# The last hidden chunk of each feed-forward as eight block products, and RWKV's key made after its triangular inverse

## Chip, core and metric

One core of one Trainium2 chip. The kernel is a single program; its time is what the device takes for one execution, in microseconds (us). TensorE (PE) multiplies matrices, VectorE (DVE) does elementwise arithmetic, ScalarE (ACT) copies and activations, GpSimd (POOL) a few small powers and masks, and SyncE (SP) issues the loads from HBM. Each works through its own queue in a fixed order and waits for the others by semaphores.

## What is computed

A decoder trunk of four layers on 256 tokens of width 1024, in float32. Each layer is a feed-forward, a token mixer and a second feed-forward, each between two RMS norms:

```python
for layer in range(DEPTH):                       # 4
    g = norm_g[layer]
    ff = swiglu(rmsnorm(h, g[0]), ffn_w_in[layer, 0], ffn_w_out[layer, 0])
    h = h + 0.5 * rmsnorm(ff, g[1])
    u = rmsnorm(h, g[2])
    m = mixer(u)          # sliding-window attention, GLA, RWKV-7, sliding-window attention
    h = h + rmsnorm(m, g[3])
    ff = swiglu(rmsnorm(h, g[4]), ffn_w_in[layer, 1], ffn_w_out[layer, 1])
    h = h + 0.5 * rmsnorm(ff, g[5])
```

`swiglu(x)` is `(silu(gate) * up) @ w_out` with `gate, up = split(x @ w_in)` and 2816 hidden columns. In RWKV-7 the key that the change moves is `k = k * (1 + (a - 1) * k_a)`, where `a` is a sigmoid of a low-rank product.

## The kernel before

The twelve stages are called 0a, 0 mixer, 0b, 1a and so on to 3b: layer, then first feed-forward, mixer, second feed-forward. The 256 tokens are two tiles of 128. Float32 products go through TensorE as three passes (`mm3`): every operand is split into a rounded high part (an ACT copy) and the rest (a DVE subtraction), and high x high, high x low and low x high are added up in PSUM.

**Feed-forward (`ffn`).** The hidden columns come in 11 chunks of 256 (`NCH`). The first three (`OLD`) go tile by tile (`tokens`), the others as *up blocks*: for each half chunk, 48 matmuls of 256 columns give gate and up for both tiles in one PSUM bank, ACT takes the SiLU, and one DVE multiplication, the *gate* (`m<-ps,hf` in the profile), makes the hidden values and frees the bank. The down product of a chunk is a 2x2 block product (two hidden halves by two output halves, for two tiles) that Strassen's scheme in Winograd's form does in seven products of three 512-column matmuls instead of eight. Each of the seven has its own PSUM bank, `acc[1]` to `acc[7]`, in which it is summed over the chunks; up blocks use the eighth bank. The scheme needs sums of blocks: `weights` makes four differences of a chunk's weight tiles and splits seven tiles, `hidden` makes four sums of hidden blocks and splits seven.

Products 1, 6, 5, 2 (`FIRST`) and 3 make tile 0's two output halves: `c1[0] = acc1 + acc2`, `c1[1] = acc1 + acc6 + acc5 + acc3`. Products 7 and 4 are wanted for tile 1 alone: in the last `TAIL` chunks they are done after tile 0's sums are recorded. `postnorm(0)` squares `c1` on ACT, multiplies it by the output norm's gain on DVE, takes a power on POOL and adds to the residual `h`; the next stage begins with a norm of `h` and TensorE transposes of it. The gain is loaded by `gain` (a row sent to all 128 partitions, 256 KB each half) and scaled on DVE (`TENSOR_SCALAR m<-m`).

**RWKV (`rwkv_unit`).** Four units, two tiles by two halves of the heads. Each makes decays, `kk`, `bt`, the key `kn` and its scaled form `kt` on DVE; then transposes, products and a triangular inverse built up over levels m = 2 to 64, in which DVE adds PSUM blocks; then `kt` is transposed (`bk[1]`) and its products with the queries' side are made.

**What sets the order.** Nothing is issued as it is written. `Recorder` records all operations with a key (TensorE work recorded so far, `base + rate * pe + shift`) and a price; `schedule` then simulates the engines and hands out in that plan each engine's order and the slots in SBUF (87 of 512 columns) and PSUM (8). Loads and splits have keys of their own windows and are pulled ahead. `nc.shift = LATE` moves the deferred products behind `postnorm(0)`. Where the plan sees TensorE wait at a boundary it puts *fillers* ahead of the waiting matmul: products of a tile `ones` by itself into the bank that comes next, whose result is never read. `emit` issues everything, so all rows of the profile carry its line: L473 for the kernel's work and L471 for fillers. A filler is one row of the order and two records in the trace.

Of the kernel before, what the change touches and what calls it, by code (L numbers as in the profile page):

```python
# [12 lines left out]
F32R = mybir.dt.float32r  # L13
# [3 lines left out]
ALU = mybir.AluOpType  # L17
# [3 lines left out]
P = 128  # L21
# [4 lines left out]
NCH = DFF // CH  # L26
NT = 2
# [130 lines left out]
LATE = 6000.0  # L158
TAIL = 4

# [322 lines left out]
class Trunk:  # L483
# [262 lines left out]
    def ffn(self, l, f, start):  # L746
# [66 lines left out]

        acc = {n: self.psum() for n in range(1, 8)}

        def products(c, which):
            w, x = wt[c], hid[c]
            for n in which:
                self.mm3(acc[n][:], x[n], tuple(v[:] for v in w[n]), c == 0, c == NCH - 1)

# [17 lines left out]
        wt, hid = {}, {}  # L838
# [14 lines left out]
        for c in range(OLD, NCH):  # L853
            for j in range(2):
# [10 lines left out]
                nc.vector.tensor_tensor(ths[c][:, j].rearrange("p t n -> p (t n)"), p[:, N:], th[:], ALU.mult)  # L865
                if j == 1:
                    wt[c] = weights(c)
                    hid[c] = hidden(ths[c])
                products(todo[0], (FIRST, SECOND if todo[0] < NCH - TAIL else SECOND[:1])[j])
            todo.pop(0)  # L870
        g = self.gain(n0 + 1, 16.0)
        for n in FIRST + SECOND[:1]:
            for c in todo:
                products(c, (n,))
        end = nc.base + nc.pe
# [10 lines left out]
        for n in SECOND[1:]:  # L886
            for c in range(NCH - TAIL, NCH):
                products(c, (n,))
        TT(u2[:], u2[:], acc[7][:], ALU.add)
        TT(c2[1][:], u4[:], acc[7][:], ALU.add)  # L890
        TT(c2[0][:], u2[:], acc[4][:], ALU.add)
# [517 lines left out]
    def rwkv_unit(self, t, l, j, rkv, hw, hg, wa2, g2, cst, out):  # L1409
# [49 lines left out]
        STT(b[:], aa[:], 1.0, kk[:], ALU.add, ALU.mult)  # L1459
        STT(aa[:], aa[:], -1.0, row("k_a")[:], ALU.add, ALU.mult)  # L1460
        STT(aa[:], aa[:], 2.0, k, ALU.add, ALU.mult)
        kn = aa
        yield
# [6 lines left out]
        STT(e2[:], kk[:], -1.0, e2[:], ALU.mult, ALU.mult)  # L1470
        bt, kt = b, e3
        STT(bt[:], b[:], 0.5, e3[:], ALU.mult, ALU.mult)
        STT(kt[:], kn[:], 0.5, e3[:], ALU.mult, ALU.mult)
        yield
# [56 lines left out]
        for m in reversed(LEVELS[:-1]):  # L1531
# [46 lines left out]
            for e in range(2):  # L1578
                right = Y[e][:].rearrange("p q (b s x) -> p q b s x", s=2, x=m)[:, :, :, 1, :]
                TT(right, right, ps[e][:, :256].rearrange("p (q b x) -> p q b x", q=4, x=m), ALU.add)  # L1580
        yield
        bk[1] = transposed(kt)
# [148 lines left out]
```

## Time and profile before

| | |
|---|---|
| median of 3 runs | 2071.83 us (2071.01 to 2072.04) |
| the profiled execution, its own time | 2070.18 us |
| its span in the trace | 2068.5 us |
| TensorE matmuls | 97% of the span busy, 13768 records |
| TensorE weight loads | 84% |
| VectorE | 89%, 3724 instructions |
| ScalarE | 65% |
| GpSimd | 6% |

A busy share says how much of the span an engine had an instruction in flight. Matmuls overlap and fillers count as busy, so 97% doesn't mean that only 3% can be had. The page's slices put the granted TensorE clock at full speed (9 tenths or more) all along.

### The profile page before, as it was taken

What the parts mean: (1) busy time and instruction counts of PE and PEld (TensorE: products, weight loads), DVE (VectorE), ACT (ScalarE), POOL (GpSimd) and SP (SyncE); (2) the same over time, 40 slices, a digit from 0 to 9 for tenths busy, and PEclk for the clock granted to TensorE, in tenths of its full rate; (3) what the DMA queues carried; (4) which work ended last, traced back from release to release, by engine and by line L of the source; (5) the groups of instructions that cost most, each with busy time, mean ns of one, the idle gap of its engine ahead of it and who ended that gap; (6) DMA issues with size and microseconds to landing.
All of it is one profiled execution on the core that took longest, in us unless ns stands there. A gap on an engine that the chain in (4) does not pass through costs nothing.

```text
span 2068.5 us, 39876 instructions
## 1 busy us (share of the span) xinstructions
PE 2008.8 (97%) x13768; PEld 1743.5 (84%) x13768; DVE 1846.5 (89%) x3724; ACT 1350.7 (65%) x2865; POOL 121.3 (6%) x185
## 2 busy tenths in 40 slices
PE   9999999999999999999999799999999999999998
PEld 7898778987898788998899677877898799877897
DVE  8998999989998998988998896678998998989996
ACT  7766577656665957666665576566765766567763
POOL 0000000002000000001100022230000000000000
PEclk9999999999999999999999999999999999999999
DMA  9666446665665455675756321455666566545662
GB/s 287 184 190 193 143 153 200 193 188 169 185 201 172 120 175 177 191 206 157 220 177 202 111 80 59 137 157 157 207 198 192 152 190 207 167 143 179 192 193 67
DMA packets 427483, 355.36 MB, mean 172 GB/s; under 512 B 32348, under 2 KB 346896, under 8 KB 427280
## 3 DMA queue, kind: packets, MB, share of 16 engines
q1 hardware_dynamic: 427280, 352.81, 56.4%
q8 instruction: 108, 1.77, 0.3%
q14 instruction: 95, 0.78, 0.1%
HBM read 351.64 MB, written 1.05 MB: 171 GB/s over the span
## 4 chain that ended last, share of the span: by engine, by line
PE 35%; DVE 9%; ACT 2%; issue 2%; DMA 2%; POOL 1%; SPq 0%; DVEq 0%; POOLq 0%; ACTq 0%
PE ps L473 35%; DVE m L473 8%; ACT m L473 1%; POOL ti L473 1%; DMA m<-in_norm_g_dram 1%; DMA m<-in_ffn_w_in_dram 1%; DVE ti L473 1%; SPq L473 0%; ACT junk L473 0%; DVE h L473 0%; POOL m L473 0%; DMA m<-in_rwkv_k_k_dram 0%; ACT hf L473 0%; ACT L473 0%; DMA m<-in_rwkv_w_o_dram 0%
## 5 line engine op out<-in xcount | busy, mean ns | idle before, releaser
L473 PE MATMUL ps<-m,m 128*128 128x256 f32 (+4 forms) x11864 | 1866.5, 322 | 33.3 <-DVE m L473 32.2
L473 PEld LDWEIGHTS ps<-m,m 128*128 128x128 f32 (+2 forms) x11864 | 1587.4, 185 | 250.3 <-DVE m L473 59.5
L473 DVE TENSOR_TENSOR m<-m,m 128x512 fp32r<-128x512 f32 (+4 forms) x2342 | 1367.3, 648 | 25.2 <-ACT m L473 20.0
L473 ACT ACTIVATE m<-m 128x512 fp32r<-128x512 f32 (+4 forms) x1838 | 1014.5, 612 | 245.1 <-DVE m L473 143.2
L473 ACT ACTIVATE hf<-ps 128x256 f32<-128x256 f32 (+1 forms) x198 | 74.8, 379 | 235.1 <-PE ps L473 232.9
L473 ACT ACTIVATE m<-ps 128x512 f32<-128x512 f32 (+3 forms) x219 | 112.2, 533 | 117.8 <-PE ps L473 112.2
L473 POOL TENSOR_TENSOR ti<-ti,nhalf 128x1 f32<-128x1 f32 (+2 forms) x60 | 51.6, 861 | 1692.3 <-DVE ti L473 1692.3
L473 DVE TENSOR_TENSOR m<-ps,hf 128x256 f32<-128x256 f32 x128 | 54.0, 422 | 53.2 <-ACT hf L473 52.0
L473 PE MATMUL ps<-ident,m 128*128 128x128 f32 (+1 forms) x472 | 79.9, 284 | 12.4 <-DVE m L473 10.2
L473 DVE TENSOR_TENSOR m<-m,ps 128x512 f32<-128x512 f32 (+1 forms) x112 | 60.6, 568 | 26.8 <-PE ps L473 24.4
L473 PEld LDWEIGHTS ps<-ident,m 128*128 128x128 f32 (+1 forms) x472 | 56.1, 144 | 32.7 <-DVE m L473 14.6
L473 ACT ACTIVATE m<-ps,gT 128x128 fp32r<-128x128 f32 (+1 forms) x192 | 53.4, 380 | 26.4 <-PE ps L473 26.3
L473 DVE TENSOR_TENSOR m<-m 128x128 f32<-128x128 f32 (+2 forms) x201 | 56.5, 321 | 3.4 <-ACT m L473 1.1
L473 DVE SCALAR_TENSOR_TENSOR m<-ps,gT,m 128x128 fp32r<-128x128 f32 x176 | 48.8, 343 | 9.8 <-ACT m L473 8.9
L473 POOL TENSOR_SCALAR_AFFINE_SELECT m<-m 128x512 f32<-128x512 f32 (+1 forms) x54 | 40.1, 762 | 190.2 <-ACT m L473 158.9
L473 ACT ACTIVATE junk<-h 128x512 bf16<-128x512 f32 x48 | 30.2, 630 | 22.9 <-DVE h L473 20.3
L473 DVE TENSOR_SCALAR m<-m 128x512 f32<-128x512 f32 (+1 forms) x36 | 13.2, 373 | 35.6 <-DMA m<-in_norm_g_dram 35.6
L473 ACT ACTIVATE junk<-m 128x512 bf16<-128x512 f32 x40 | 25.0, 625 | 28.3 <-DVE m L473 24.6
L473 DVE SCALAR_TENSOR_TENSOR h<-m,ti,h 128x512 f32<-128x512 f32 x48 | 34.0, 747 | 4.8 <-POOL ti L473 4.6
L473 DVE TENSOR_TENSOR m<-ps,m 128x512 f32<-128x512 f32 (+1 forms) x44 | 29.6, 686 | 8.6 <-ACT m L473 4.0
L473 PEld LDWEIGHTS ps<-hf,m 64*128 64x128 f32 (+1 forms) x592 | 30.1, 169 | 6.1 <-ACT m L473 2.9
L471 PE MATMUL ps<-ones 128*128 128x128 f32 x262 | 34.7, 279 | 0.0
(91 smaller groups left out, 577.2 us busy)
## 6 DMA issues: line engine op xcount, KB each, us to landing
m<-in_ffn_w_in_dram SPq DMA_DIRECT2D x1024, 128.0 KB, 2.9
m<-in_ffn_w_out_dram SPq DMA_DIRECT2D x352, 256.0 KB, 4.1
m<-in_ffn_w_in_dram SPq DMA_DIRECT2D x192, 256.0 KB, 3.9
m<-in_swa_w_qkv_dram SPq DMA_DIRECT2D x48, 256.0 KB, 3.7
m<-in_rwkv_w_rkv_dram SPq DMA_DIRECT2D x48, 256.0 KB, 3.0
m<-in_gla_w_in_dram SPq DMA_DIRECT2D x40, 256.0 KB, 3.0
m<-in_swa_w_o_dram SPq DMA_DIRECT2D x32, 256.0 KB, 3.3
m<-in_norm_g_dram SPq DMA_DIRECT2D x24, 256.0 KB, 4.7
```

The lines of the kernel that those rows point to most:

```text
L471: self.nc.tensor.matmul(fix(o.tiles[0][:, :P]), lhsT=x, rhs=x, start=True, stop=True)
L473: getattr(getattr(self.nc, o.eng), fn)(*[fix(v) for v in args], **{k: fix(v) for k, v in kw.items()})
```

## The change

Three edits.

1. In every feed-forward the last chunk leaves the seven-product scheme. Its weights are four plain tiles, split without differences, and its hidden values one tile, split at once. `plain(0)` adds tile 0's four block products (12 matmuls) to `acc[2]` and `acc[3]`; `plain(1)`, recorded after `postnorm(0)`, adds tile 1's four (12) to `acc[4]` and a new `acc[8]`. The other four sums end with the last chunk but one. Tile 1's second half becomes `c2[1] = acc1 + acc6 + acc5 + acc7 + acc8`, one addition more.
2. `TAIL` goes from 4 to 3, so products 7 and 4 are deferred for the chunks 8 and 9 and no longer for chunk 7.
3. In RWKV the three DVE instructions that make `kn` and `kt` are recorded after the inverse, and with them the load of the row `k_a`.

```diff
--- before.py
+++ after.py
@@ -156,7 +156,7 @@
 OLD = 3
 WARMUP = 9
 LATE = 6000.0
-TAIL = 4
+TAIL = 3
 
 AHEAD = 8000.0
 RESERVE = 16
@@ -811,12 +811,20 @@
             return {n: tuple(v[:, m, :] for v in z) for n, z, m in (
                 (1, x, 2), (2, x, 0), (4, x, 1), (5, y, 0), (6, y, 1), (7, y, 2), (3, y, 3))}
 
-        acc = {n: self.psum() for n in range(1, 8)}
+        acc = {n: self.psum() for n in range(1, 9)}
 
         def products(c, which):
             w, x = wt[c], hid[c]
             for n in which:
-                self.mm3(acc[n][:], x[n], tuple(v[:] for v in w[n]), c == 0, c == NCH - 1)
+                self.mm3(acc[n][:], x[n], tuple(v[:] for v in w[n]), c == 0, c == NCH - 2 and n not in (2, 3, 4))
+
+        def plain(t):
+
+            for i in range(2):
+                o = acc[(2, 3, 4, 8)[2 * t + i]]
+                for j in range(2):
+                    w = wt[NCH - 1][j, i]
+                    self.mm3(o[:], tuple(v[:, j, t, :] for v in hid[NCH - 1]), (w.hi, w.lo), (t, i, j) == (1, 1, 0), j == 1)
 
         def tokens(t, c):
 
@@ -863,15 +871,15 @@
                 th = self.hf([P, N])
                 nc.scalar.activation(th[:], p[:, :N], AF.Silu)
                 nc.vector.tensor_tensor(ths[c][:, j].rearrange("p t n -> p (t n)"), p[:, N:], th[:], ALU.mult)
-                if j == 1:
-                    wt[c] = weights(c)
-                    hid[c] = hidden(ths[c])
+                if j == 1 and c < NCH - 1:
+                    wt[c], hid[c] = weights(c), hidden(ths[c])
+                elif j == 1:
+                    wt[c] = {(z, i): self.weight(w_out[:, 2 * c + z, i * 512:(i + 1) * 512]) for z in range(2) for i in range(2)}
+                    hid[c] = split(ths[c][:], lambda: self.m2([P, 2, NT, P], F32R))
                 products(todo[0], (FIRST, SECOND if todo[0] < NCH - TAIL else SECOND[:1])[j])
             todo.pop(0)
         g = self.gain(n0 + 1, 16.0)
-        for n in FIRST + SECOND[:1]:
-            for c in todo:
-                products(c, (n,))
+        plain(0)
         end = nc.base + nc.pe
         s1, u2, u4 = self.m2(), self.m2(), self.m2()
         c1, c2 = self.pair(), self.pair()
@@ -884,10 +892,12 @@
         self.postnorm(0, [x[:] for x in c1], g)
         nc.base, nc.pe, nc.shift = end, 0.0, LATE
         for n in SECOND[1:]:
-            for c in range(NCH - TAIL, NCH):
+            for c in range(NCH - TAIL, NCH - 1):
                 products(c, (n,))
+        plain(1)
         TT(u2[:], u2[:], acc[7][:], ALU.add)
-        TT(c2[1][:], u4[:], acc[7][:], ALU.add)
+        TT(u4[:], u4[:], acc[7][:], ALU.add)
+        TT(c2[1][:], u4[:], acc[8][:], ALU.add)
         TT(c2[0][:], u2[:], acc[4][:], ALU.add)
         self.postnorm(1, [x[:] for x in c2], g)
         nc.shift = 0.0
@@ -1457,9 +1467,6 @@
         nc.gpsimd.tensor_tensor(s[:, :8], s[:, :8], self.nhalf[:, :8], ALU.pow)
         TT(h8(kk[:]), h8(kk[:]), b8(s), ALU.mult)
         STT(b[:], aa[:], 1.0, kk[:], ALU.add, ALU.mult)
-        STT(aa[:], aa[:], -1.0, row("k_a")[:], ALU.add, ALU.mult)
-        STT(aa[:], aa[:], 2.0, k, ALU.add, ALU.mult)
-        kn = aa
         yield
 
         e1, e2, e3 = self.m2(), self.m2(), self.m2()
@@ -1468,9 +1475,8 @@
         ACT(e2[:], e2[:], AF.Exp)
         ACT(e1[:], pc[:], AF.Exp)
         STT(e2[:], kk[:], -1.0, e2[:], ALU.mult, ALU.mult)
-        bt, kt = b, e3
+        bt, kt, kn = b, e3, aa
         STT(bt[:], b[:], 0.5, e3[:], ALU.mult, ALU.mult)
-        STT(kt[:], kn[:], 0.5, e3[:], ALU.mult, ALU.mult)
         yield
 
         def transposed(x):
@@ -1578,6 +1584,9 @@
             for e in range(2):
                 right = Y[e][:].rearrange("p q (b s x) -> p q b s x", s=2, x=m)[:, :, :, 1, :]
                 TT(right, right, ps[e][:, :256].rearrange("p (q b x) -> p q b x", q=4, x=m), ALU.add)
+        STT(kn[:], kn[:], -1.0, row("k_a")[:], ALU.add, ALU.mult)
+        STT(kn[:], kn[:], 2.0, k, ALU.add, ALU.mult)
+        STT(kt[:], kn[:], 0.5, e3[:], ALU.mult, ALU.mult)
         yield
         bk[1] = transposed(kt)
         AK = pairs(0, 1)
```

In numbers, from the orders of both kernels: TensorE has 24 matmuls of 512 columns more (21 to 24 in each of eight last chunks) and its fillers at stage boundaries and in RWKV go from 131 to 79. Per boundary they go from 7 to 1 at the end of 0a and of 3a, 20 to 15 at 0b, 1b and 2b, 10 to 1 at 1a, 12 to 11 at 2a, none before or after at 3b, and 25 to 10 inside RWKV (the other ten stay). VectorE has 88 instructions less (11 in each feed-forward, seven of them of 512 columns), ScalarE 32 less.

Three places show what moves. In the rows, the engine's instruction is followed by what it writes and reads (buffers by running numbers, which differ between the kernels) and its size.

**TensorE at the end of 0b, right after its last up block.** Before (`ps_105` is `acc[1]`, `ps_109` is `acc[2]`, `ps_110` to `ps_112` are `acc[3]`, `acc[7]`, `acc[4]`; `m_1401` to `m_1406` are the last hidden chunk's blocks):

```order
L473 MATMUL ps_111_4400<-m_1333_6062,m_1354_6177 128x512
L473 MATMUL ps_111_4400<-m_1303_5917,m_1355_6185 128x512
L473 MATMUL ps_112_4412<-m_1207_5486,m_1255_5700 128x512
L473 MATMUL ps_105_4332<-m_1331_6057,m_1401_6380 128x512
L473 MATMUL ps_105_4332<-m_1368_6243,m_1401_6380 128x512
L473 MATMUL ps_109_4373<-m_1340_6107,m_1401_6380 128x512
L473 MATMUL ps_105_4332<-m_1331_6057,m_1402_6387 128x512
L473 MATMUL ps_109_4373<-m_1374_6262,m_1401_6380 128x512
L473 MATMUL ps_109_4373<-m_1340_6107,m_1402_6387 128x512
L473 MATMUL ps_112_4412<-m_1222_5551,m_1255_5700 128x512
L473 MATMUL ps_106_4342<-m_1372_6256,m_1404_6395 128x512
L473 MATMUL ps_106_4342<-m_1382_6285,m_1404_6395 128x512
```

After (`ps_110`, `ps_111`, `ps_112`, `ps_113` are `acc[2]`, `acc[3]`, `acc[7]`, `acc[4]`; `m_1388`, `m_1389` are the last chunk's split hidden values):

```order
L473 MATMUL ps_112_4370<-m_1290_5887,m_1349_6173 128x512
L473 MATMUL ps_113_4382<-m_1246_5695,m_1294_5909 128x512
L473 MATMUL ps_113_4382<-m_1261_5760,m_1294_5909 128x512
L473 MATMUL ps_113_4382<-m_1246_5695,m_1295_5916 128x512
L473 MATMUL ps_110_4343<-m_1318_6011,m_1388_6354 128x512
L473 MATMUL ps_110_4343<-m_1337_6101,m_1388_6354 128x512
L473 MATMUL ps_111_4358<-m_1319_6018,m_1388_6354 128x512
L473 MATMUL ps_111_4358<-m_1338_6108,m_1388_6354 128x512
L473 MATMUL ps_113_4382<-m_1298_5934,m_1345_6144 128x512
L473 MATMUL ps_110_4343<-m_1318_6011,m_1389_6362 128x512
L473 MATMUL ps_110_4343<-m_1322_6031,m_1388_6354 128x512
L473 MATMUL ps_110_4343<-m_1341_6121,m_1388_6354 128x512
```

Before, 15 matmuls of the last chunk (products 1, 2, 6, 5, 3) stand between the last up block and the end of tile 0's sums, and three of product 7 behind them; now `plain(0)`'s 12 stand there, and products 1, 6, 5, 2 of the chunk before have all gone ahead of the last up block. Behind the last up block there are 36 matmuls before the fillers where there were 37, and ahead of it, back to the up block before the last but one, four more.

**VectorE at the same place, from the last gate on.** Before (`m_1400` and `m_1403` on are hidden sums and splits, the row that writes `m_1410` is `c1[0]`, `m_1417` is `c1[1]`):

```order
L473 TENSOR_TENSOR m_1373_6258<-ps_128_6287,hf_44_6371 128x256
L473 TENSOR_TENSOR m_1400_6378<-m_1373_6258 128x128 x2
L473 TENSOR_TENSOR m_1400_6378<-m_1400_6378,m_1373_6258 128x128
L473 TENSOR_TENSOR m_1402_6387<-m_1373_6258,m_1401_6380 128x384
L473 TENSOR_TENSOR m_1400_6378<-m_1373_6258,m_1400_6378 128x128
L473 TENSOR_TENSOR m_1403_6393<-m_1378_6274,m_1381_6283 128x512
L473 TENSOR_TENSOR m_1406_6402<-m_1400_6378,m_1404_6395 128x512
L473 TENSOR_TENSOR m_1410_6413<-m_1405_6399,ps_109_4373 128x512
L473 TENSOR_TENSOR m_1412_6420<-m_1410_6413,m_1323_6032 128x512
L473 TENSOR_TENSOR m_1414_6428<-m_1405_6399,ps_106_4342 128x512
L473 TENSOR_TENSOR m_1416_6436<-m_1414_6428,ps_107_4350 128x512
L473 TENSOR_TENSOR m_1417_6441<-m_1416_6436,ps_110_4388 128x512
```

After (`m_1370` and `m_1371` are `u2` and `u4`, `m_1389` the hidden split, `m_1392` and `m_1395` weight splits, `m_1396` is `c1[0]` and `m_1398` is `c1[1]`):

```order
L473 TENSOR_TENSOR m_1366_6244<-ps_129_6269,hf_44_6347 128x256
L473 TENSOR_TENSOR m_1370_6256<-m_1370_6256,ps_112_4370 128x512
L473 TENSOR_TENSOR m_1389_6362<-m_1366_6244,m_1388_6354 128x512
L473 TENSOR_TENSOR m_1392_6371<-m_1390_6365,m_1391_6367 128x512
L473 TENSOR_TENSOR m_1395_6382<-m_1393_6378,m_1394_6380 128x512
L473 TENSOR_TENSOR m_1396_6385<-m_1367_6247,ps_110_4343 128x512
L473 TENSOR_TENSOR m_1397_6390<-m_1396_6385,m_1320_6021 128x512
L473 TENSOR_TENSOR m_1398_6397<-m_1371_6261,ps_111_4358 128x512
L473 TENSOR_TENSOR m_1399_6402<-m_1398_6397,m_1321_6028 128x512
L473 TENSOR_TENSOR m_1371_6261<-m_1371_6261,ps_112_4370 128x512
L473 SCALAR_TENSOR_TENSOR ti_55_6412<-ti_54_6393 128x1
```

The hidden sums are gone, `u2` and `u4` have been added before the last gate (behind the one before it), and two weight splits stand between the gate and `c1[0]`.

**VectorE in RWKV, one unit's `kn` and `kt`.** Before, in the preparation of the units (`m_3599` is `kn`, `m_3565` is `bt`, `m_3605` is `kt`'s scale):

```order
L473 SCALAR_TENSOR_TENSOR m_3565_16200<-m_3599_16348,m_3563_16196 128x512
L473 SCALAR_TENSOR_TENSOR m_3604_16372<-m_3521_15987,q_8_15860,m_3518_15959 128x128
L473 SCALAR_TENSOR_TENSOR m_3599_16348<-m_3599_16348,m_3547_16099 128x512
L473 SCALAR_TENSOR_TENSOR m_3565_16200<-m_3565_16200,m_3605_16376 128x512
L473 SCALAR_TENSOR_TENSOR m_3599_16348<-m_3599_16348,m_3543_16079 128x512
L473 TENSOR_TENSOR m_3607_16393<-ps_314_16363,m_3596_16340 128x512
L473 TENSOR_TENSOR m_3611_16403<-ps_316_16386,m_3540_16069 128x512
L473 TENSOR_TENSOR m_3614_16413<-ps_317_16388,m_3548_16101 128x512
L473 SCALAR_TENSOR_TENSOR m_3607_16393<-m_3563_16196,m_3607_16393 128x512
L473 TENSOR_SCALAR m_3611_16403<-m_3611_16403 128x512
L473 SCALAR_TENSOR_TENSOR m_3592_16315<-m_3614_16413,m_3588_16302 128x512
L473 SCALAR_TENSOR_TENSOR m_3605_16376<-m_3599_16348,m_3605_16376 128x512
```

After, `kn` and `kt` at the end of the inverse of tile 0's units (`m_3531`, `m_3548` are two units' `kn`, `m_3542`, `m_3550` their `kt`; the additions `128x8x32` and `128x4x64` are the inverse's last levels):

```order
L473 TENSOR_TENSOR m_3227_14697<-m_3227_14697,ps_432_17540 128x16x16
L473 SCALAR_TENSOR_TENSOR m_3531_16194<-m_3531_16194,m_3703_17558 128x512
L473 SCALAR_TENSOR_TENSOR m_3531_16194<-m_3531_16194,m_3474_15921 128x512
L473 SCALAR_TENSOR_TENSOR m_3548_16265<-m_3548_16265,m_3707_17594 128x512
L473 SCALAR_TENSOR_TENSOR m_3542_16236<-m_3531_16194,m_3542_16236 128x512
L473 TENSOR_TENSOR m_3176_14466<-m_3176_14466,ps_436_17584 128x8x32
L473 TENSOR_TENSOR m_3178_14474<-m_3178_14474,ps_437_17586 128x8x32
L473 SCALAR_TENSOR_TENSOR m_3548_16265<-m_3548_16265,m_3516_16139 128x512
L473 TENSOR_TENSOR m_3714_17634<-m_3531_16194,m_3592_16531 128x512
L473 SCALAR_TENSOR_TENSOR m_3550_16291<-m_3548_16265,m_3550_16291 128x512
L473 TENSOR_TENSOR m_3166_14433<-m_3166_14433,ps_438_17622 128x4x64
L473 TENSOR_TENSOR m_3167_14436<-m_3167_14436,ps_439_17624 128x4x64
```

Twelve such instructions leave the preparation and come after it, among the levels of the inverse and right behind it.

## Rows read from the trace of the kernel before

**Rows 1.** The page's first part: busy us, share, instructions of each engine.

```profile
PE 2008.8 (97%) x13768; PEld 1743.5 (84%) x13768; DVE 1846.5 (89%) x3724; ACT 1350.7 (65%) x2865; POOL 121.3 (6%) x185
```

**Rows 2.** Groups by form: count | busy us, mean ns | idle before, releaser.

```profile
L473 PE MATMUL ps<-m,m 128*128 128x256 f32 x6216 | 769.5, 282 | 22.5 <-DVE m L473 22.5
...
L471 PE MATMUL ps<-ones 128*128 128x128 f32 x262 | 34.7, 279 | 0.0
```

**Rows 3.** PE's timeline, end of 0b: start, us, what, count [wait, releaser].

```profile
435.78 7.36 PE L473 MATMUL ps<-m,m 128*128 128x256 f32 x54 [0.21 <-DVE m L473]
444.27 22.94 PE L473 MATMUL ps<-m,m 128*128 128x256 f32 x145 [1.13 <-DVE m L473]
467.05 4.63 PE L471 MATMUL ps<-ones 128*128 128x128 f32 x40
471.87 1.11 PE L473 MATMUL ps<-ident,m 128*128 128x128 f32 x8 [0.20 <-DVE m L473]
```

**Rows 4.** PE's timeline elsewhere: three matmuls of 512 columns, and one.

```profile
200.16 0.96 PE L473 MATMUL ps<-m,m 128*128 128x512 f32 x3 [0.18 <-ACT m L473]
...
1369.26 0.50 PE L473 MATMUL ps<-m,hf 128*128 128x512 f32 x1
```

**Rows 5.** VectorE's timeline at 0b, from the last gate to the next stage's norm.

```profile
459.09 0.42 DVE L473 TENSOR_TENSOR m<-ps,hf 128x256 f32<-128x256 f32 x1 [0.19 <-ACT hf L473]
...
459.96 2.35 DVE L473 TENSOR_TENSOR m<-m,m 128x128 f32<-128x128 f32 x5
462.22 0.68 DVE L473 TENSOR_TENSOR m<-m,ps 128x512 f32<-128x512 f32 x1
...
463.55 2.86 DVE L473 TENSOR_TENSOR m<-m,ps 128x512 f32<-128x512 f32 x4
...
466.93 0.15 DVE L473 SCALAR_TENSOR_TENSOR ti<-ti 128x1 f32<-128x1 f32 x1
467.00 1.28 DVE L473 TENSOR_TENSOR m<-m,ps 128x512 f32<-128x512 f32 x2
468.19 1.41 DVE L473 SCALAR_TENSOR_TENSOR h<-m,ti,h 128x512 f32<-128x512 f32 x2
...
471.33 0.88 DVE L473 TENSOR_SCALAR m<-h,ti 128x512 f32<-128x512 f32 x2 [0.66 <-POOL ti L473]
```

**Rows 6.** ScalarE's timeline there: the last up block's SiLU, and `c1[1]`'s square.

```profile
458.67 0.39 ACT L473 ACTIVATE hf<-ps 128x256 f32<-128x256 f32 x1 [1.22 <-PE ps L473]
...
465.85 0.63 ACT L473 ACTIVATE junk<-m 128x512 bf16<-128x512 f32 x1 [1.61 <-DVE m L473]
```

**Rows 7.** VectorE's timeline at the very end: tile 1's `h`.

```profile
2063.66 1.42 DVE L473 SCALAR_TENSOR_TENSOR h<-m,ti,h 128x512 f32<-128x512 f32 x2 [0.73 <-POOL ti L473]
```

**Rows 8.** VectorE's timeline at 0b, around the gain's load.

```profile
434.96 0.43 DVE L473 TENSOR_SCALAR m<-m 128x512 f32<-128x512 f32 x1 [5.33 <-DMA m<-in_norm_g_dram]
...
435.64 6.10 DVE L473 TENSOR_TENSOR m<-m,m 128x512 fp32r<-128x512 f32 x10
...
443.80 0.42 DVE L473 TENSOR_TENSOR m<-ps,hf 128x256 f32<-128x256 f32 x1
```

**Rows 9.** Waits of the whole execution: total us, times, longest.

```profile
DVE m L473 <- DMA m<-in_norm_g_dram: 35.6, 7, 5.7
```

**Rows 10.** VectorE's timeline in RWKV's preparation: three of the moved kind.

```profile
1205.48 1.89 DVE L473 SCALAR_TENSOR_TENSOR m<-m,m 128x512 f32<-128x512 f32 x3
```

**Rows 11.** Windows, end of 2a and RWKV: us, PE, PEld, DVE, ACT, POOL busy, clock.

```profile
1155.00:1160.00 5.00, 2.39 (x21) 2.16 (x19) 2.82 (x7) 1.52 (x6) 1.10 (x2) 1.00 0.88 280
1160.00:1165.00 5.00, 5.00 (x22) 4.45 (x22) 3.88 (x22) 3.12 (x12) 0.00 (x0) 0.66 0.23 77
1178.00:1199.00 21.00, 19.04 (x112) 13.99 (x112) 21.00 (x65) 11.46 (x26) 5.17 (x5) 1.00 0.54 167
1199.00:1235.00 36.00, 35.01 (x248) 25.41 (x250) 35.63 (x66) 25.91 (x54) 6.50 (x7) 1.00 0.16 50
1260.00:1300.00 40.00, 39.33 (x489) 31.95 (x488) 20.65 (x50) 24.34 (x59) 10.40 (x18) 1.00 0.19 61
1300.00:1340.00 40.00, 39.92 (x494) 32.80 (x495) 25.49 (x52) 22.63 (x51) 5.85 (x8) 1.00 0.46 144
```

**Rows 12.** PE's timeline in RWKV, after the inverse.

```profile
1375.96 0.63 PE L473 MATMUL ps<-ident,m 128*128 128x128 f32 x4 [2.66 <-DVE m L473]
...
1378.59 0.44 PE L473 MATMUL ps<-ident,hf 128*128 128x128 f32 x2 [0.93 <-DVE hf L473]
```

**Rows 13.** PE's timeline at the end of 2a: the transposes after its fillers.

```profile
1159.95 1.88 PE L473 MATMUL ps<-ident,m 128*128 128x128 f32 x8 [2.61 <-DVE m L473]
```

## The prediction

> **What bounds the kernel now.** I read the page's first part, then the groups by form, then each engine's timeline at one feed-forward's end, then windows over RWKV. TensorE has a matmul in flight for 2008.8 of 2068.5 us [rows 1], so the rest, 59.7 us, is the smaller part of what can be had. Two things hide in the busy share. One is fillers: 262 records, 131 fillers [rows 2], and the 40 records that stand at the end of 0b take 4.63 us [rows 3], so a filler is a wait of 4.63 / 20 = 0.23 us that counts as work. All of them are some 30 us. The other is VectorE, 89% busy, which is what TensorE waits for.
>
> At the end of a feed-forward the bound changes from TensorE to a chain. I call the end of the last up block at 0b T; ScalarE's SiLU starts there, at 458.67 [rows 6]. TensorE then works off 37 matmuls until 467.05 and fills until 471.87 [rows 3]. Meanwhile VectorE goes from the gate (T + 0.4) through hidden sums and splits (the five instructions from 459.96 to 462.31) to `c1[0]` at 462.22 and the four additions of `u2`, `u4`, `c1[1]` and `acc[7]` from 463.55 on [rows 5]. The square of `c1[1]` starts at 465.85 [rows 6], so that `c1[1]` is there at T + 7.2; the power's input follows at 466.93, `h` at 468.19, the next norm's scaling at 471.33 [rows 5] and the next stage's transposes at 471.87 [rows 3]. A step of this chain that goes comes back one for one until TensorE's own 36 or 37 matmuls (8.4 us) are the later ones.
>
> In RWKV's preparation VectorE is the bound: busy 21.00 of 21.00 and 35.63 of 36.00 us from 1178 to 1235, and 20.65 and 25.49 of 40 later, from 1260 to 1340, where TensorE has 39.33 and 39.92 [rows 11].
>
> **The change, part by part. More matmuls.** Matmuls of 512 columns start (0.96 - 0.50) / 2 = 0.23 us apart [rows 4], so 24 more are 24 x 0.23 = +5.5 us of TensorE. By the order four more per feed-forward lie ahead of the last up block and one less behind it. The four (0.92 us) stand just where TensorE waits for the gate that frees its bank: 1.13 us at 0b ahead of the last but one up block [rows 3], 22.5 us over all up blocks [rows 2], 2.8 us for each of eight feed-forwards. The gate is late since it is queued behind the gain's scaling, which waits 5.33 us for its load, and ten and three weight splits of 0.61 us (the next gate is at 443.80, 8.8 us after the scaling's start) [rows 8]; seven such waits make 35.6 us [rows 9]. The four matmuls move none of that, so I cost them at nothing. If the cover is gone they cost up to 0.92 x 8 = +7.4 us.
>
> **The shorter chain at a boundary.** Behind the gate there now stand `u2 += acc[7]`, one hidden split, two weight splits, `c1[0]`, its gain product and `c1[1]`. TensorE does nine matmuls of older chunks, then `plain(0)`'s 12 with one other among them: 22 x 0.23 = 5.1 us, so `acc[3]` ends at T + 5.1. VectorE's five instructions up to the splits' end are 0.42 + 4 x 0.61 plus a wait for ScalarE's 0.6 us copy, that is to T + 3.9, so the products are the later. `c1[0]` can go while `acc[3]` is finished, and `c1[1]` ends at about T + 5.1 + 0.7 to T + 6.4, against T + 7.2. Between the power's input and `h` one tile-1 addition of 0.6 us goes too, of which at most 0.4 counts, because POOL's power needs its 0.73 us of wait after the 0.15 us instruction [rows 7] and `h` came 1.26 us after the input's start [rows 5]. Sum: -0.8 to -1.4 from the first, -0.4 to 0 from the second; I take -1.1. The plan drops five fillers here (20 to 15), 5 x 0.23 = 1.15 us, which is the same.
>
> That lets me price the others by their fillers: 0b, 1b and 2b 3 x -1.1 = -3.3; 0a and 3a lose six each, 2 x -1.4 = -2.8; 1a loses nine, -2.1; 2a one, -0.2; at 3b there is no next stage, and only the shorter way to the last `h` counts, -0.5. Together **-8.9**. Bounds: 0 if in each place another wait comes in, and -13 (1.6 at each of eight) if each boundary gets both ends of its sum. I take -9.
>
> What is removed beside it hides: seven 512-column instructions of VectorE per feed-forward, 7 x 0.61 x 8 = 34 us, lie mostly where TensorE is the bound, and come back only through earlier gates. Those are part of the cover above. The eighth sum takes a PSUM bank that the evacuated sums have left, which I cost at nothing: tile 0's additions have emptied three by then. Should it wait, it is `plain(1)` that waits, six matmuls before the fillers.
>
> **RWKV's key.** Twelve instructions of 0.60 us ((1.89 - 0.69) / 2 by the three in a row, with 0.69 for one) [rows 5, 10] leave VectorE's full stretch: 7.2 us. They land from the end of tile 0's inverse on, where VectorE has about 19 and 15 us to spare in 40 [rows 11]. `k_a`'s loads go behind seventeen weight loads on SP's queue and are wanted some 100 us later, so they cost nothing. TensorE can give back only what it doesn't use: fillers in RWKV go from 25 to 10, 15 x 0.23 = 3.5 us; idle time of 1.96 and 0.99 us from 1178 to 1235 [rows 11]; and two waits after the inverse of 2.66 and 0.93 us [rows 12], which can shrink if the inverse starts earlier, or grow, since `kt`'s transpose now hangs on instructions that run late. 3.5 + 0.4 x 6.5 is about **-6**. Bounds: 0 (VectorE's queue is as late at the inverse's end as before) and -10 (3.5 + 6.5).
>
> **The sum.** 2070.2 (the profiled execution's own time) - 9 - 6 = 2055.2. The median lies 1.65 us above that execution: 2056.8, **2057 us**, 0.7% faster.
>
> **The rivals.**
>
> *A: only the boundaries gain.* The moved key's twelve instructions meet the inverse's additions in VectorE's queue, and what the preparation wins is lost there. For it: the inverse alternates TensorE and VectorE, and the two waits of [rows 12] are on VectorE. Against: 20 of 40 us are free. 2071.8 - 9 = 2062.8 us. With the boundaries' gain gone as well (an input norm or a load comes last instead), some 2070.
>
> *B: the four matmuls aren't covered.* If the gain's load lands sooner, the gate frees the bank sooner and the 0.92 us are paid in seven or eight places: the boundaries' -9 becomes -2, and with RWKV's -6 that is 2063.8 us. For it: the waits differ among feed-forwards (22.5 us in eight, not 1.13 each [rows 2, 3]). Against: VectorE's queue behind the gain stays 13 instructions long.
>
> *C: slower.* TensorE is the bound at every feed-forward's end and the dropped fillers are replaced by waits of the same length: `c1[1]` is not earlier than T + 7.2, because the two weight splits and the hidden split stand ahead of it on VectorE and are late (their loads or ScalarE's copies). Then nothing pays for 5.5 us of matmuls, RWKV gives nothing, and the time is 2077.4 us. It decides from the point where those splits end after T + 6. For it: 0.61 us each, and ScalarE waits among them. Against: their loads are issued far ahead.
>
> *D: the clock.* With fewer fillers TensorE idles longer at boundaries. At the end of 2a, after a wait of 2.61 us behind its fillers [rows 13], the granted clock of the next 5 us was 0.66 [rows 11], so between its levels of 1.2 and 2.4 GHz; everywhere else in those windows it was 1.00. Such a dip costs 0.34 x 5 = 1.7 us; at seven boundaries 12 us, and the sum is 2068.9. It decides if an unfilled wait as long as that one appears elsewhere. Against: fillers go only where the plan sees the wait gone, and 15 of 20 stay at 0b. The Trainium skill's page "TensorE: Matmul & The Clock Gate" (Part 1: The HAM clock gate) says the same mechanism, a gate set by how busy the array was recently, and so speaks against dropping fillers; the trace agrees at 2a's end with 0.66.
>
> **How the numbers follow.** Forecast 0.47; A 0.17; B 0.10; both of A's losses together 0.10; C 0.12; D 0.04. A measurement of this kernel can tell about 0.2%, 4.1 us, from no change: faster is below 2067.7, slower above 2076.0. Faster takes the forecast, A and B, 0.74; same takes 2070 and D, 0.14; slower is C, 0.12. The range reaches from 2046 (the boundaries' -13 and RWKV's -10 would be 2048.8, and 2 us below for what frees up earlier) to 2070, which leaves out C and the outer part of the rest.
>
> **What would show it.** Right: some 158 records of fillers; the time from the last up block's end to the next stage's first transposes at 0b down from 13.2 to about 12.1 us; TensorE's wait ahead of the last but one up block at 0b shrunk from 1.13 us to a few tenths with that block starting no later; VectorE no longer full in RWKV's preparation and the stretch to the inverse shorter by 3 us or more. Wrong: that wait unchanged and the up blocks later (B); a wait on VectorE ahead of the transposes as long as the fillers dropped (C); a new wait of over 2 us ahead of `kt`'s transposes (A); granted clock below 1.00 behind a boundary other than 2a's (D). It would also be wrong if the four matmuls push a load's buffer so that a later chunk's split is late, which I have not priced.

## The result

The changed kernel takes 2040.49 us (median of 4 runs, 2038.24 to 2043.70) against 2071.42 us beside it: a ratio of 0.9853, 95% interval 0.9835 to 0.9871. It is faster by 31 us where 14.8 were forecast, and lies 5.5 us below the range. The profiled execution has a span of 2036.5 us. Its page and groups by form (columns as in [rows 1, 2]):

```profile
PE 1997.1 (98%) x13688; PEld 1738.2 (85%) x13688; DVE 1809.3 (89%) x3636; ACT 1336.2 (66%) x2833; POOL 118.6 (6%) x185
```
```profile
L473 PE MATMUL ps<-m,m 128*128 128x256 f32 x6216 | 769.2, 282 | 9.7 <-DVE m L473 9.5
...
L471 PE MATMUL ps<-ones 128*128 128x128 f32 x158 | 20.4, 277 | 0.0
```

Fillers are 158 records, as the order had them. TensorE's wait ahead of up-block matmuls has fallen from 22.5 us [rows 2] to 9.7. To see where the time went I cut both traces at TensorE's landmarks: the end of each last up block (T) and each next stage's first transposes.

| | forecast | measured |
|---|---|---|
| eight feed-forwards up to T | 0 | -7.1 |
| of these: 1a, 2a, 3a | 0 | -6.6 |
| of these: 0a, 0b, 1b, 2b, 3b | 0 | -0.5 |
| eight ends, T to the next transposes (3b: to the end) | -8.9 | -11.3 |
| GLA | 0 | -1.9 |
| RWKV | -6 | -11.6 |
| both attention stages | 0 | 0.0 |

TensorE's timeline at the end of 0b (T is 457.12; start, us, what, count, wait), to be laid beside [rows 3]:

```profile
442.71 22.73 PE L473 MATMUL ps<-m,m 128*128 128x256 f32 x144 [0.42 <-DVE m L473]
465.28 3.51 PE L471 MATMUL ps<-ones 128*128 128x128 f32 x30
468.97 1.09 PE L473 MATMUL ps<-ident,m 128*128 128x128 f32 x8 [0.19 <-DVE m L473]
```

The transposes are at T + 11.85, they were at T + 13.24. Behind them stands VectorE's chain, and ScalarE's square of `c1[1]` (last row), against [rows 5, 6]:

```profile
461.32 0.69 DVE L473 TENSOR_TENSOR m<-m,ps 128x512 f32<-128x512 f32 x1 [0.28 <-PE ps L473]
...
464.58 0.15 DVE L473 SCALAR_TENSOR_TENSOR ti<-ti 128x1 f32<-128x1 f32 x1
464.65 0.68 DVE L473 TENSOR_TENSOR m<-m,ps 128x512 f32<-128x512 f32 x1
465.39 1.41 DVE L473 SCALAR_TENSOR_TENSOR h<-m,ti,h 128x512 f32<-128x512 f32 x2
```
```profile
463.37 0.63 ACT L473 ACTIVATE junk<-m 128x512 bf16<-128x512 f32 x1 [0.60 <-DVE m L473]
```

`c1[0]` now waits for TensorE (0.28 us), `c1[1]` is there at T + 6.2 instead of T + 7.2, and one tile-1 addition stands between the power's input and `h` instead of two. That is the mechanism of the forecast.

The forecast held VectorE's queue around the gain's load fixed, and it has changed, as these rows show beside [rows 8, 9] (the last is of the waits of the whole execution):

```profile
427.74 4.30 DVE L473 TENSOR_TENSOR m<-m,m 128x512 fp32r<-128x512 f32 x7 [0.15 <-ACT m L473]
433.40 0.43 DVE L473 TENSOR_SCALAR m<-m 128x512 f32<-128x512 f32 x1 [1.35 <-DMA m<-in_norm_g_dram]
...
435.01 7.31 DVE L473 TENSOR_TENSOR m<-m,m 128x512 fp32r<-128x512 f32 x12
442.24 0.42 DVE L473 TENSOR_TENSOR m<-ps,hf 128x256 f32<-128x256 f32 x1
```
```profile
DVE m L473 <- DMA m<-in_norm_g_dram: 7.3, 6, 1.5
```

The load isn't faster: relative to T it is issued at about -28 and the scaling starts at -23.7 in both kernels. But eight instructions of 512 columns stand between the gate before and the scaling (the first row has seven, all splits) where there were two, and VectorE does them while the load is under way. Before, this one stood last ahead of its wait of 5.33 us:

```profile
428.94 0.69 DVE L473 TENSOR_TENSOR m<-m,m 128x512 fp32r<-128x512 f32 x1 [0.16 <-ACT m L473]
```

This brings the gate at 0b no nearer to the load. It comes 8.84 us behind the scaling in both kernels (443.80 - 434.96 [rows 8] and 442.24 - 433.40). TensorE waits less there (0.21 and 1.13 us before [rows 3], 0.42 after) and the whole stretch of 0b up to T is only 0.4 us shorter: the added matmuls stand where TensorE waited.

Nearly all that the stretches ahead of T won, 6.6 of 7.1 us, was won in 1a, 2a and 3a, the feed-forwards that follow another, and there at the first two gates, some 110 us ahead of T. TensorE's timeline at 1a, before and then after:

```profile
511.60 18.71 PE L473 MATMUL ps<-m,m 128*128 128x512 f32 x103
531.62 5.97 PE L473 MATMUL ps<-m,m 128*128 128x256 f32 x48 [1.31 <-DVE m L473]
538.57 3.70 PE L473 MATMUL ps<-m,m 128*128 128x256 f32 x29 [0.98 <-DVE m L473]
```
```profile
509.58 27.63 PE L473 MATMUL ps<-m,m 128*128 128x512 f32 x178
```

Both waits are gone. In the three feed-forwards together they were 7.2 us. By the orders, VectorE had 73 instructions of 512 columns between tile 0's new `h` at the end of 0b and 1a's first gate, and has 68.

### The profile page after: what moved, and what is told of

The parts are those of the page before. It is cut to its first block, busy times and chain, and to the rows that moved or that the text cites. A ratio compares the mean times of both kernels' runs of the same rounds, so it can differ in the third digit from the quotient of the medians.

```text
span 2036.5 us, 39630 instructions
## 1 busy us (share of the span) xinstructions
PE 1997.1 (98%) x13688; PEld 1738.2 (85%) x13688; DVE 1809.3 (89%) x3636; ACT 1336.2 (66%) x2833; POOL 118.6 (6%) x185
## 4 chain that ended last, share of the span: by engine, by line
PE 75%; DVE 15%; ACT 3%; DMA 3%; issue 2%; POOL 2%; SPq 0%; DVEq 0%; POOLq 0%; ACTq 0%
PE ps L473 75%; DVE m L473 13%; DMA m<-in_ffn_w_in_dram 2%; POOL ti L473 2%; ACT m L473 2%; ACT junk L473 1%; DVE ti L473 1%; DVE h L473 1%; ACT L473 0%; DVE hf L473 0%; DMA m<-in_ffn_w_out_dram 0%; DMA m<-in_norm_g_dram 0%; SPq L473 0%; ACT hf L473 0%; DMA m<-in_swa_b_qkv_dram 0%
## 5 line engine op out<-in xcount | busy, mean ns | idle before, releaser
L473 PE MATMUL ps<-m,m 128*128 128x256 f32 (+5 forms) x11888 | 1869.4, 322 | 15.9 <-DVE m L473 13.9
L473 DVE TENSOR_TENSOR m<-m,m 128x512 fp32r<-128x512 f32 (+3 forms) x2262 | 1326.0, 650 | 29.4 <-ACT m L473 23.7
L473 ACT ACTIVATE m<-m 128x512 fp32r<-128x512 f32 (+3 forms) x1806 | 996.3, 612 | 221.9 <-DVE m L473 127.9
L473 DVE TENSOR_TENSOR m<-m,ps 128x512 f32<-128x512 f32 (+1 forms) x120 | 66.9, 577 | 27.4 <-PE ps L473 25.1
L473 PE MATMUL ps<-ident,m 128*128 128x128 f32 (+1 forms) x472 | 78.9, 284 | 11.3 <-DVE m L473 9.3
L473 DVE TENSOR_TENSOR m<-m 128x128 f32<-128x128 f32 (+3 forms) x185 | 52.8, 325 | 2.8 <-ACT m L473 0.8
L473 ACT ACTIVATE junk<-m 128x512 bf16<-128x512 f32 x40 | 25.5, 637 | 34.4 <-DVE m L473 31.7
L473 PE MATMUL ps<-hf,m 64*128 64x64 f32 (+1 forms) x592 | 34.5, 259 | 0.5 <-ACT m L473 0.4
L473 DVE SCALAR_TENSOR_TENSOR m<-m,q,m 128x128 f32<-128x128 f32 x96 | 30.4, 369 | 0.0
```

The costliest lines, as they stand in the source:

```text
L473: getattr(getattr(self.nc, o.eng), fn)(*[fix(v) for v in args], **{k: fix(v) for k, v in kw.items()})
```

## The experiments

All are edits of one of the two kernels. "Up" (the feed-forwards up to T) and the other columns are changes against the kernel before, cut as above in one profiled execution of each (us); "gain" is VectorE's wait for the gain's load. The runs of one kernel lie up to 6 us apart, those of the changed kernel 5.5, so a difference of 4 us from its median is at the edge of what four runs can tell.

| | median | up | ends | GLA | RWKV | gain |
|---|---|---|---|---|---|---|
| before | 2071.4 | 0 | 0 | 0 | 0 | 35.6 |
| after | 2040.5 | -7.1 | -11.3 | -1.9 | -11.6 | 7.3 |
| e1 feed-forward edits alone | 2049.5 | -4.5 | -11.2 | -2.0 | -3.7 | 9.1 |
| e2 key's move alone | 2062.4 | +2.3 | -0.4 | 0.0 | -7.0 | 37.5 |
| e3 after, TAIL 4 | 2052.2 | +0.9 | -10.6 | -0.4 | -8.5 | 36.0 |
| e4 after, dead work | 2044.4 | -5.5 | -10.3 | -1.4 | -9.2 | 7.1 |
| e5 before, TAIL 3 | 2062.5 | -1.6 | +2.0 | -3.2 | -6.5 | 4.1 |
| e6 after, TAIL 2 | 2043.4 | -0.2 | -5.7 | -3.8 | -16.4 | 4.0 |
| e7 after, 83 buffers | 2060.7 | +14.2 | -9.7 | -0.7 | -12.3 | 34.4 |
| e8 after, gain early | 2033.1 | -10.5 | -11.9 | -2.0 | -13.4 | 0 |
| e9 before, gain early | 2060.2 | -10.0 | +0.4 | 0.0 | -1.0 | 0 |
| e10 after, no fillers | 2044.6 | -3.9 | -11.2 | -1.9 | -8.6 | 8.9 |
| e11 e8 with 88 buffers | 2039.7 | -8.1 | -11.9 | -1.9 | -6.2 | 0 |
| e12 e8, TAIL 2 at 2a | 2033.5 | -9.1 | -11.3 | -1.9 | -14.7 | 0 |
| e13 before, TAIL 3 and key | 2059.6 | -1.3 | +2.3 | -3.2 | -8.8 | 7.6 |
| e14 e8, 12 small buffers | 2032.6 | -9.9 | -11.9 | -2.0 | -13.7 | 0 |
| e15 before, 83 buffers | 2073.5 | -2.0 | +2.5 | +3.2 | -0.1 | 0 |
| e16 e8, `k_a` early | 2033.7 | -10.4 | -11.9 | -2.0 | -12.5 | 0 |

"Up" adds up different places. Here it is by feed-forward (0a with what stands ahead of it), and beside it TensorE's waits (us) ahead of up-block matmuls: at the last gates, within 25 us of T, in all eight feed-forwards, and at the first gates of 1a, 2a and 3a. The first gates of the other five have 7.6 us before and 6.8 to 8.5 in all these runs.

| | 0a, 0b, 1b, 2b, 3b | 1a, 2a, 3a | waits at the last gates | at the first gates of 1a, 2a, 3a |
|---|---|---|---|---|
| before | 0 | 0 | 7.6 | 7.2 |
| after | -0.5 | -6.6 | 2.0 | 0 |
| e1 | +1.9 | -6.4 | 5.0 | 0 |
| e3 | +0.5 | +0.4 | 6.9 | 5.1 |
| e4 | +2.1 | -7.6 | 3.6 | 0 |
| e5 | -0.5 | -1.2 | 2.6 | 2.6 |
| e6 | -0.3 | 0.0 | 0.5 | 2.6 |
| e8 | -3.8 | -6.8 | 0 | 0 |
| e9 | -7.4 | -2.6 | 0.2 | 5.6 |
| e15 | -7.6 | +5.6 | 0 | 7.5 |

In e2, which leaves the feed-forwards alone, the two parts are +0.7 and +1.5; differences of that size say little.

**The parts alone.** e1 puts the key's three lines back to where they were, e2 moves only them:

```diff
 # e1, against the changed kernel, behind b = (aa + 1) * kk (e2: the reverse, on the kernel before)
+        STT(aa[:], aa[:], -1.0, row("k_a")[:], ALU.add, ALU.mult)
+        STT(aa[:], aa[:], 2.0, k, ALU.add, ALU.mult)
...
+        STT(kt[:], kn[:], 0.5, e3[:], ALU.mult, ALU.mult)
```

> The changed kernel with RWKV's key made early again, as before. Cut at TensorE's landmarks, the changed kernel's 32.0 us fall on: feed-forwards up to their last up block 7.2, from there to the next stage's first transposes 11.3, GLA 1.9, RWKV 11.6. Theory 1, each part is the work of its own edit: RWKV's stretch is as before (250.2 us from the end of 2a to its own end) and the rest stays, 2070.2 - 20.3 = 2050 us. Rival: RWKV is shorter mostly because feed-forward 2a leaves VectorE less behind, so the stretch keeps 5 us or more of the 11.6 without the edit: 2045 us or less.

> The kernel before with the key made behind the inverse and nothing else. Theory 1 (parts add up): the stretch of RWKV loses 11.6 us, 2058.5 us. Rival (2a's backlog on VectorE is what counts): 6 us or less, 2064 us or more.

The key's move gives RWKV 7.0 us by itself, near the 6 of the forecast. The feed-forward edits give it another 3.7 and GLA 2.0, without a line of either stage changed. Neither theory of the expectations is whole: 7.0 + 3.7 is 0.9 short of 11.6.

**Is it TAIL, or VectorE's lighter load?** e3 is `-TAIL = 3` `+TAIL = 4`. e4 adds

```diff
+                    nc.kind = "split"
+                    for n in range(7):
+                        d = self.m2()
+                        nc.vector.tensor_tensor(d[:], wt[c][n % 2, n // 2 % 2].hi, wt[c][n // 2 % 2, n % 2].lo, ALU.subtract)
+                    nc.kind = None
```

> The changed kernel with TAIL 4 again: products 7 and 4 of chunk 7 (six matmuls, 1.4 us) stand behind tile 0's sums once more and fill the time in which TensorE waits for them. If the plain last chunk does the work and TAIL is only a matter of taste, within 2 us of the changed kernel, 2038 to 2043 us. If the deferral of less work is part of the gain (the six matmuls ahead of the last up block hide behind its waits), 2045 us or more. Its plan has ten fillers less, 69 for 79, which would make it faster by 2.3 us if the fillers count one for one.

> The changed kernel with seven dead VectorE subtractions of 128x512 on each last chunk's weights, whose results nothing reads: 56 instructions of 0.61 us, 34 us of VectorE's time come back; the plan's fillers stay at 79. Theory R (relief: the feed-forwards' stretches up to the last up block and GLA's gained 9.1 us since VectorE has less to do): those stretches are back at the time before or nearly, 2047 us or more. Rival Q (queue: they gained since the gain's scaling no longer stands ahead of the gates while its load is under way): no more than 2 us slower than the changed kernel, as long as the scaling stays where it is.

With all of VectorE's removed time put back (34 us), the median is 3.9 us higher, with runs that overlap the changed kernel's, and "up" keeps -5.5: relief is the smaller part. With TAIL 4 the ends keep -10.6 but "up" and GLA lose all or most they had won, and the gain's wait is 36.0 us again. So the plain chunk makes the ends. The stretches ahead of T need both edits: in 1a, 2a and 3a the plain chunk without TAIL 3 gives +0.4 us (e3), TAIL 3 without the plain chunk -1.2 (e5, below) and the two together -6.4 (e1). e3 is slower than the changed kernel though its plan has ten fillers less.

**Buffers or places?** e5 is TAIL 3 on the kernel before, e6 TAIL 2 on the changed one, e7 `"m2": (512, 83)`.

> The kernel before with TAIL 3 and nothing else: seven products in the last chunk as before, six matmuls of chunk 7's products 7 and 4 moved ahead. Theory S (slots): the buffers that chunk 7's deferred products held are free earlier, so VectorE has fewer of the next stage's splits left behind tile 0's new h (73 of 512 columns until the first gate of 1a before, 68 in the changed kernel, 70 here): the two waits of TensorE at the first gates of 1a, 2a and 3a (2.6 to 2.9 us each) shrink by half or more, and so does the gain's wait of 35.6 us; the ends of the feed-forwards gain nothing. About 2071.4 - 6 = 2065 us. Rival (TAIL helps only together with the plain chunk): within 2 us of the kernel before, or slower.

> The changed kernel with TAIL 2: six more matmuls ahead of the last up block in each feed-forward, six fewer behind it. By theory S the first gates stay as in the changed kernel (67 splits for 68), but behind the last up block TensorE runs out of work 1.4 us earlier and waits (its plan has 99 fillers, 20 more), and the six matmuls ahead are paid as far as no wait is left there: 0 to +1.4 us per feed-forward, 2040 to 2051 us, centre 2046. Rival (less deferred is better still): below 2038 us.

> The changed kernel with 83 instead of 87 buffers of 512 columns, nothing else. Theory S: what TAIL 3 won was buffers, so with four fewer the splits left until the first gate of 1a, 2a and 3a go from 68 to 70 and the stretches up to the last up block lose 1 to 2.5 us in each of the three, with some more in GLA and RWKV: 2040.5 + 7 = 2047 us, and the chain behind the last up block stays at -1.4 us. Rival (an accident of the order, not buffers): within 2 us of the changed kernel.

e5 takes the gain's wait from 35.6 to 4.1 us without the plain chunk. Yet "up" wins only 1.6 us, since the matmuls that are deferred no longer now stand ahead of T: 27 more than before in the trace, some 6 us at 0.23 us each. Most of e5's 8.9 us came in RWKV and GLA. In e6 the gain's wait is as small and "up" wins nothing. Four buffers fewer cost the changed kernel 20 us (e7), and the wait is back:

```profile
DVE m L473 <- DMA m<-in_norm_g_dram: 34.4, 7, 5.8
```

TensorE's wait ahead of up-block matmuls is 26.2 us there. The 20 us are far more than the 7 that theory S (buffers decide) gave them, so I took the wait away by itself (e8, e9; shortened here) and the buffers from the kernel before (e15).

```diff
         for c in range(OLD, NCH):
+            if c == NCH - 1:
+                g = self.pair()   # and the two loads of the gain's row, kind "load"
...
-        g = self.gain(n0 + 1, 16.0)
+        for x in g:   # kind "split"
+            nc.vector.tensor_scalar(x[:], x[:], 16.0, None, ALU.mult)
```

> The changed kernel with the output gain's load issued before the last chunk's up blocks, some 20 us earlier, and scaled where it was. If the last gates still wait for it, the remaining 7.3 us of waits on that load go and TensorE's waits of 0.25 to 1.3 us ahead of the last but one up block shrink: 2 to 4 us faster, 2036 to 2038 us. If VectorE is full there without it, nothing changes: 2039 to 2042 us.

> The kernel before with the output gain's load issued ahead of the last chunk's up blocks and scaled where it was. The 35.6 us of VectorE's waits on that load go. If they held the last gates back (as my sum had it), TensorE's waits at the last two gates, 0.9 to 1.3 us in seven feed-forwards, go too and nothing pays them back: 6 to 8 us faster, 2064 us. If buffers are what counts (theory S), the two buffers that the early load holds cost about what it wins: within 3 us of the kernel before.

> The kernel before with 83 large buffers. If buffers bind it as they bind the changed kernel (four were worth 20 us there), 2085 to 2095 us, most of it in the feed-forwards up to the last up block. If the gain's wait was the whole of it (it is there already with 87), within 5 us of the kernel before.

Taken away alone, the wait is worth 10.9 us in the kernel before (2071.1 to 2060.2), nearly all of it in "up": it does hold the gates. But e9 wins it mostly in 0a, 0b, 1b, 2b and 3b (-7.4), where the changed kernel won 0.5. Early loads give the changed kernel another 7.4 us, 3.3 of them in those five, and e8 is faster than both kernels (ratio 0.9815, 0.9800 to 0.9830).

With 83 buffers the kernel before is 2.1 us slower, within the noise (ratio 0.9998 to 1.0017), where theory S as I had put it gave 14 or more. That doesn't refute it, because two effects cancel in e15. In its plan the scaling lies behind other work and the wait is 0, which wins 7.6 us in the five feed-forwards as in e9; and 1a, 2a and 3a lose 5.6, GLA 3.2 and the ends 2.5. Beside e9, which has no such wait either, e15 is 13 us slower. So buffers cost, and the place of the scaling in VectorE's queue moves with them and with TAIL, not in one direction. How much of e7's 20 us is which I did not separate.

Buffers go together with how many splits are left for the first gates. Instructions of 512 columns up to 1a's first gate, and TensorE's excess over its usual pace at the first two gates there: 78 in e15, 1.70 and 1.21 us; 73 before, 1.48 and 1.14; 72 in e3, 0.99 and 1.16; 70 in e5, 0 and 1.10; 68 after and in e4, none. The count isn't all: e6 has 67, and 0 and 1.10 us. Over 1a, 2a and 3a the excess is 8.2 us before and 0.3 after.

**The clock.** e10 leaves the fillers out: `for _ in range(0)`.

> The changed kernel without any filler (79 left out, 18 us of them on TensorE); all else in the same order. Rival D (the clock): waits at the boundaries go unfilled and the granted clock falls to about 0.66 for some 5 us behind each, 1.7 us each: 10 to 15 us slower, 2050 us or more, with the clock below 1.00 in windows behind 0b, 1b and 2b. If the clock doesn't mind waits of 3.5 us: within 2 us of the changed kernel.

Its median is 4.2 us higher. Behind 0b TensorE waits 3.53 us unfilled and the windows from 465 to 475 are (columns as in [rows 11]: the granted clock stands behind POOL's), e10 and then the changed kernel:

```profile
465.00:470.00 5.00, 1.47 (x8) 0.99 (x7) 3.09 (x7) 2.06 (x6) 1.10 (x2) 0.81 0.75 242
470.00:475.00 5.00, 5.00 (x16) 4.12 (x15) 3.39 (x11) 4.57 (x13) 0.00 (x0) 0.50 0.00 0
```
```profile
465.00:470.00 5.00, 4.81 (x40) 4.36 (x39) 2.79 (x6) 2.40 (x8) 0.91 (x2) 1.00 0.68 225
470.00:475.00 5.00, 4.98 (x21) 3.77 (x21) 4.16 (x13) 5.00 (x16) 0.05 (x1) 1.00 0.01 3
```

The mechanism of rival D is real, 0.50 being the lower of the two levels. Of the 0.19 x 5 + 0.50 x 5 = 3.4 us of clock lost in these windows, partly while TensorE waited, the stretch of 1a lost 1.5 (its "up" is -0.8 here and -2.3 in the changed kernel). That is near D's 1.7 us for one dip. But few places pay as much: 2a, behind 1b with 0.66 of the clock from 963 to 968, lost 0.4. So D's 12 us for the whole are too high.

**Can more be had, and what is RWKV's share?** e11 is e8 with 88 large and 12 small buffers, e14 with 87 and 12, e12 with TAIL 2 in 2a alone, e16 with `row("k_a")` recorded where it was; e13 is TAIL 3 and the key's move on the kernel before.

> The changed kernel with the gain's load early and one buffer of 512 columns more (88), paid for with two of the fourteen 256-column ones. Theory S: four buffers fewer cost 20 us, so one more is worth 1 to 5: 2028 to 2032 us against 2033.1 with the early load alone. If the 256-column buffers were needed, 2035 us or more.

> The changed kernel with the gain's load early and twelve instead of fourteen 256-column buffers, 87 large ones. If the missing small buffers cost RWKV its 7 us in e11, the stretch is 243 to 245 us here too and the time 2039 us or more. If the other order of e11 did it, RWKV is at 237 to 239 us and the time 2033 to 2035 us.

> The changed kernel with the gain's load early, and TAIL 2 in feed-forward 2a alone, the one ahead of RWKV. TAIL 2 everywhere made RWKV 4.7 us shorter than in the changed kernel, and 2a with its boundary 2.2 us longer. If this holds by itself, 2 to 3 us faster than the early load alone, 2030.5 us; if RWKV's gain came from what lay before 2a, no gain or 1 to 2 us slower, 2033 to 2035 us.

> The changed kernel with the gain's load early and the row k_a loaded where its load was recorded before, its use staying behind the inverse. VectorE's wait of 1.4 us for k_a goes; if TensorE waited for it, 1 to 2 us faster than with the early gain alone, 2031.5 us; four rows' buffers are held some 100 us longer, which would cost 2 us or more if RWKV is short of buffers: 2035 us or more.

> The kernel before with TAIL 3 and the key made behind the inverse, the seven products kept. If RWKV's 11.6 us are TAIL's 6.5 and the key's 7.0 (theory: VectorE's backlog at the end of 2a, then its preparation), the stretch loses 11 to 13 us without the plain chunk: 2062.5 - 6 = 2056 us. If the plain chunk is needed, it loses 7 to 9: 2060 us.

One buffer more makes it 6.5 us slower, in RWKV, and e14 shows that the small buffers aren't the cause: it is the order that comes out. e12, e14 and e16 are not told apart from e8. In e13 RWKV gains 8.8, less than the 13.5 of its two parts alone, and within the 7 to 9 that were expected if the plain chunk is needed.

## Why the prediction was wrong

- **The shorter chain: right, 2.4 us too small.** At 0b -1.4 against -1.1, with `c1[1]` and `h` where the working had them. The step that was off is "price the others by their fillers": 2a, one filler less, gave -1.2 instead of -0.2, 3b -1.6 instead of -0.5, and 1a, nine less, only -1.2 instead of -2.1. The chain is the same everywhere; fillers say what the plan saw, not what is won.
- **What stands ahead of T, costed at nothing: the step that failed.** "The four matmuls move none of that, so I cost them at nothing", and the removed VectorE work was "part of the cover above". The prediction gave all of TensorE's 22.5 us at the gates to the feed-forwards alike, 2.8 each, behind the gain's load, and held them there as cover for the added matmuls. By place, only 7.6 us stood at the last gates; 7.2 stood at the first gates of 1a, 2a and 3a, and 7.6 at those of the other five. The cover at the last gates did what it was meant for: those waits fell by 5.7 us, 27 more matmuls stand ahead of T, TensorE is busy 3.7 us longer there, and the five feed-forwards that follow no other came out at -0.5. What had no term is that the first gates' 7.2 us go, and with them 6.6 us of time. It takes TAIL 3 and the plain chunk together (e1 against e3 and e5).
- **The gain's wait** fell from 35.6 to 7.3 us, which the prediction held fixed too, but that is not where the time came from: at 0b the gate is as far behind the scaling as it was. e9's 10.9 us say what the wait is worth when no matmuls take its place.
- **RWKV's key: right by itself** (7.0 for 6). What had no term is that a feed-forward's edit changes the mixer behind it: the feed-forward edits alone gave RWKV 3.7 and GLA 2.0. Less work left over on VectorE is a likely reason and in part seen: in the profiled executions the inverse's first instruction on VectorE came 72.1 us behind 2a's transposes before, 70.1 in e1, 70.0 in e2, and 64.8 after.
- **"Comes back only through earlier gates"** for the 34 us of removed VectorE work: about right, 3.9 us by e4, at the edge of the noise.
- **Rivals.** A is refuted by e2. B did not happen in the changed kernel: the load lands no sooner and the cover held (-0.5 us in the five feed-forwards). Its mechanism shows in e8 beside e9: with the load early there is next to no wait left at the last gates, and the kernel with the added matmuls wins 3.8 us in the five where the one without wins 7.4. C is refuted by `c1[1]` at T + 6.2. D needs long unfilled waits at more places. The changed kernel has one, of 3.88 us inside RWKV, with 0.93 and 0.73 of the clock in the 10 us from 1159 to 1169, where the kernel before had 0.66 in 5 us behind 2a; e10 made more. The Trainium skill's page "TensorE: Matmul & The Clock Gate" (Part 1: The HAM clock gate) has an array that was idle run at half its clock; the 0.50 of e10 agrees.

Together the misses make up the difference between 15 and 32 us in the profiled executions: 7.1 ahead of T, 5.6 in RWKV, 2.4 at the ends, 1.9 in GLA.

What stays open: which buffer or price in the plan puts the scaling ahead of or behind the other work and takes the first gates' waits away, and why RWKV's gain, with the key's move the same, lies anywhere from 6.2 (e11) to 16.4 us (e6). I tried no kernel in which RWKV's order is held fixed.

## What to carry to other kernels

When an order is made by a planner, compare the place of every instruction that waits for a load, not only of those the diff names: one short instruction that arrives 5 us before its data holds everything behind it on its engine. Try that wait alone first (load earlier, use where it was); it gave 10.9 us on the old kernel and 7.4 on the new. But a wait that shrinks isn't time won: here VectorE's waits for the gain fell by 28 us and at the gates behind them the time went to matmuls that had moved there. Sort a total of waits by place before calling it cover, and cut both traces at the same landmarks to see where the time went. An edit's price is looked for in the next stage too: the feed-forward edits gave the two mixers behind them 5.7 us (e1).

## What was not expected of the hardware

Where TensorE waited 3.53 us between two busy stretches, the granted clock was 0.81 in the 5 us from 465, which hold the wait, and 0.50 in the next 5 (e10), yet the whole kernel lost only 4.2 us of its median without any of its 79 fillers.
